# Both MLP matrices by Strassen's seven products: the second one too, with its split combinations of features written to DRAM by the first

## The chip, the cores and the metric

One core of a Trainium2 chip runs the whole program. Its engines are TensorE (PE, with its weight loads, PEld), VectorE (DVE), ScalarE (ACT), GpSimd (POOL) and SyncE (SP, which here only issues transfers); 16 DMA engines move data between DRAM and the on-chip SBUF. Matmul results go to PSUM, here eight banks of 128 x 512 fp32. The metric is device time of one execution in microseconds, less is better.

## The reference

One block of a sequence model: x is 512 tokens of 2048 features. Two mixers (HGRN2 and Hyena, not touched here) are followed by an MLP with a squared relu, and a final RMS norm:

```python
def _sq_relu_mlp(u, w1, w2):
    return jnp.square(jax.nn.relu(u @ w1)) @ w2

x = x + g1 * mix_lat
x = x + g2 * _sq_relu_mlp(_modulate(_rmsnorm(x, norm2_g[layer]), sh2, sc2), w_mlp1[layer], w_mlp2[layer])
...
return _rmsnorm(x, final_norm_g)
```

`w_mlp1` is 2048 x 8192, `w_mlp2` is 8192 x 2048, all in fp32. h = relu(u w1)² has 8192 features for each of 512 tokens.

## The kernel before

**Precision.** Every fp32 operand is split into a high part (a cast to fp32r on ScalarE) and a low part (the rest, a subtraction on VectorE). A product is three matmuls: high x high, high x low, low x high (`mm3`, L265-268). Weights come as pieces of 128 x 1024 (512 KB) on SP's queue; `wsplit` (L214-220) makes `whi` (ScalarE, L218) and `wlo` (VectorE, L161, the line of every tensor-tensor operation) in three buffers each. `take` (L1188) hands the next split piece to PE and calls `ahead`, which emits the splits three pieces on; the table `loads` says at which piece which transfer is issued.

**First matrix, feature-major.** h comes in 32 sets of 256 features. Set 0 is plain. For sets 1 to 31 the product of the 2 x 2 blocks of w1 and of x is made by Strassen's scheme with seven products instead of eight: P1, P2, P6, P5, P7, P3, P4, each 8 x 3 = 24 matmuls of 128 x 256, thus 168 a set. The combinations of x (tiles `U`, seven for each of 8 feature groups) are made once before the loop, by `u_plain` and `u_sums` (L1082-1092: casts L1079, L1089, sums `cb` L1088, differences L161). The sums of weights (`wsum`, `raw<-raw`) are made for each set on VectorE. The four results of a set come from PSUM through `s` (copies on ScalarE) and `c` (sums on VectorE), and `store_h` (L1200) squares them and stores the set as fp32, 512 KB, to `hd[s]` on ScalarE's queue.

**Second matrix, plain.** Two passes over the features, one for each half of the 2048 outputs. A step `q` reads one set of h back (`load_h`, L1172, SP's queue, 512 KB), splits it (`hs`: ScalarE L1280, VectorE L161), takes two weight pieces (`load_w2`, `prep_w2`) and makes 4 token blocks x 2 halves x 2 x 3 = 48 matmuls of 128 x 512 in `down` (L1294-1304); 64 steps. The eight banks sum over a whole pass. `evacuate` (L1306) then makes x + g2 · result, and `final` (L1284) the norm and the stores.

**Order.** The program is written in one order and each engine runs its own instructions in that order; a wait in front of one instruction holds all behind it on that engine. The tile framework places semaphores and moves nothing but by the positions of `take` and the hooks.

Of the kernel before, what the change touches and what calls it, by code (L numbers as in the profile page):

```python
# [154 lines left out]
def body(nc, tc, A, out, stack, dbg, stop):  # L155
# [38 lines left out]
    hd = [DR.tile([P, 1024], F32, name=f"hd{s_}") for s_ in range(DFF // 256)]  # L194
# [870 lines left out]
    def u_plain(q):  # L1065

        ca = cas[q] = ca_tile(q)
        for j in range(2):
            kb = 2 * q + j
            xp = bank(2 * (q % 2) + j)  # L1070
            for i in range(4):
                pe.transpose(xp[:, i * P:(i + 1) * P], x1[i][:, kb * P:(kb + 1) * P], ident)
            act.activation(out=ca[:, 2 * j:2 * j + 2].rearrange("p a t -> p (a t)"), in_=xp, func=AF.Identity,
                           scale=gn2[:, kb:kb + 1], bias=sh2[:, kb:kb + 1])
        if q == 7:
            close("R")
            pools["X"] = pool("X", side=right)
        u = U[q] = (UP if q < 7 else pools["X"]).tile([P, 2, 7, 256], F32R, tag=f"u{q}", name=f"u{q}")
        act.copy(u[:, 0, 0:4], ca)  # L1079
        tt(u[:, 1, 0:4], ca, u[:, 0, 0:4].bitcast(F32), ALU.subtract)  # L1080

    def u_sums(q):  # L1082

        ca, u = cas.pop(q), U[q]
# [4 lines left out]
        act.copy(u[:, 0, 4:7], cb[:, 0:3])  # L1089
        tt(u[:, 1, 4:7], cb[:, 0:3], u[:, 0, 4:7].bitcast(F32), ALU.subtract)  # L1090
        act.copy(u[:, 0, 0], cb[:, 3])
        tt(u[:, 1, 0], cb[:, 3], u[:, 0, 0].bitcast(F32), ALU.subtract)
# [27 lines left out]

    def prep_set(s):
# [18 lines left out]
        def p3():  # L1140
            tt(st[1], st[1], raws[s][1], ALU.add)
            return split(st[1])
        return [lambda: split(raws[s][0]), lambda: split(raws[s][1]), p6, lambda: split(st[0]), p7, p3,
                lambda: split(raws[s][3])]


    w2 = mlp2_order()
    N1 = 7 * (NS - 1)
    WLAST = 4
    preps = [f for s in range(1, NS) for f in prep_set(s)]  # L1150
    loads = {7 * (s - 2): [lambda s=s: load_set(s)] for s in range(2, NS)}
    raw2, hraw = {}, {}

    def load_w2(t):
        if t < 2:
            raw2[t] = YM.tile([P, 1024], F32, tag=f"ym{8 + t}", name="w2raw")
        else:
            raw2[t] = wraw()
        dma(raw2[t], A["tiles"][mlp_tile[w2[t]]])

    def prep_w2(t):
        raw = raw2.pop(t)
        if t < len(w2) - WLAST:
            hi, lo = wsplit(raw)
        else:
            hi = pools["V"].tile([P, 1024], F32R, tag=f"xhi{t % WLAST}", name="xhi")
            lo = pools["V"].tile([P, 1024], F32R, tag=f"xlo{t % WLAST}", name="xlo")
            act.copy(hi, raw)
            tt(lo, raw, hi.bitcast(F32), ALU.subtract)
        return tuple(v.rearrange("p (k n) -> p k n", k=2) for v in (hi, lo))  # L1170

    def load_h(q):  # L1172
        hraw[q] = pools["X"].tile([P, 2, 512], F32, tag=f"hr{q % 2}", name="hraw")
        dma(hraw[q].rearrange("p a t -> p (a t)"), hd[q % NS])

    preps += [lambda t=t: prep_w2(t) for t in range(len(w2))]
    for t in range(len(w2)):
        loads.setdefault(7 * (NS - 2) if t < 2 else N1 + t - 3, []).append(lambda t=t: load_w2(t))
    for q in range(2 * NS):
        loads.setdefault(7 * (NS - 2) if q < 1 else N1 + 2 * q - 4, []).append(lambda q=q: load_h(q))  # L1180
# [7 lines left out]
    def take():  # L1188
        g = at[0]
        for f in loads.pop(g, ()):  # L1190
            f()
# [4 lines left out]
    def c_tile():  # L1196
        return YM.tile([P, 4, 256], F32, tag=f"ym{12 + c_tile.n % 2}", name="c")
    c_tile.n = 0

    def store_h(s, c):  # L1200

        act.activation(out=c, in_=c, func=AF.Square)
        mdma(hd[s], c.rearrange("p a t -> p (a t)"))
        c_tile.n += 1
# [4 lines left out]
    for q in range(8):  # L1209
# [19 lines left out]
    c = c_tile()  # L1229
# [4 lines left out]
    def xs_(tag):  # L1234
        return pools["X"].tile([P, 256], F32, tag=tag, bufs=2, name=tag)

    def product(ps, name, start):
        hi, lo = take()
        i = SLOT[name]
        for q in range(8):  # L1240
            mm3(ps, hi[:, q], lo[:, q], U[q][:, 0, i], U[q][:, 1, i], start and q == 0, q == 7)

    for s in range(1, NS):
        X, Y, Z = (bank(3 * (s % 2) + i)[:, 0:256] for i in range(3))
        c = c_tile()
# [12 lines left out]
        tt(c[:, 2], X, s5, ALU.add)
        act.activation(out=c[:, 2], in_=c[:, 2], func=AF.Relu, scale=-1.0)
        product(Z, "P3", False)  # L1260
        tt(c[:, 0], Z, s2, ALU.add)
        act.activation(out=c[:, 0:2], in_=c[:, 0:2], func=AF.Relu)
        product(X, "P4", False)
        act.activation(out=c[:, 3], in_=X, func=AF.Relu, scale=-1.0)
        store_h(s, c)


    close("U")
    pools["V"] = pool("V")
    rows2 = [YM.tile([P, 2, 512], F32, tag=f"ym{12 + ng}", name="rows2") for ng in range(4)]  # L1270
    grs = [t[:, 0] for t in rows2]
    ss3 = pools["V"].tile([P, 4, 4], F32, name="ss3")
    x1 = [pools["V"].tile([P, D], F32, name=f"x1b{i}") for i in range(4)]
    hs = {}

    def split_h(q):
        for j in range(2):
            pl, tag, nb_ = (YM, f"ym{10 + j}", 1) if q == 0 else (pools["V"], f"hs{j}", 3)
            t = pl.tile([P, 2, 512], F32R, tag=tag, bufs=nb_, name="hs")
            act.copy(t[:, 0], hraw[q][:, j])  # L1280
            tt(t[:, 1], hraw[q][:, j], t[:, 0].bitcast(F32), ALU.subtract)
            hs[q, j] = t

    def final(i0):  # L1284

        r = rstd(pools["V"], ss3[:, i0:i0 + 2], 2, f"r3{i0}")
        for ng in range(4):
            for i in range(2):
                sl = slice(ng * 512, (ng + 1) * 512)
                t = x1[i0 + i][:, sl]  # L1290
                vec.scalar_tensor_tensor(out=t, in0=t, scalar=r[:, i:i + 1], in1=rows2[ng][:, 1], op0=ALU.mult, op1=ALU.mult)
                dma(out[0, (i0 + i) * P:(i0 + i + 1) * P, sl], t)

    def down(q, w_, toks):  # L1294
        for g, (hi, lo) in enumerate(w_):
            for i in toks:
                sl = slice(i * P, (i + 1) * P)
                ps = psb[4 * g + i]
                for j in range(2):
                    t = hs[q, j]  # L1300
                    first, last = q % NS == 0 and j == 0, q % NS == NS - 1 and j == 1
                    pe.matmul(ps, t[:, 0, sl], hi[:, j], start=first, stop=False, skip_group_check=True)  # L1302
                    pe.matmul(ps, t[:, 0, sl], lo[:, j], start=False, stop=False, skip_group_check=True)  # L1303
                    pe.matmul(ps, t[:, 1, sl], hi[:, j], start=False, stop=last, skip_group_check=True)  # L1304

    def evacuate(p, toks):  # L1306
        for g in range(2):
            for i in toks:
                residual(pools["V"], psb[4 * g + i], i, 2 * p + g, ss3)

    split_h(0)
    NL, late = WLAST // 2, []
    for q in range(2 * NS):
        if q % NS == 0:
            psb = [bank(i) for i in range(8)]
        if q + 1 < 2 * NS:
            split_h(q + 1)
        if q == 1:
            for ng in range(4):
                sl = slice(ng * 512, (ng + 1) * 512)  # L1320
                mdma(rows2[ng][:, 0], grow[1:2, sl].broadcast_to([P, 512]))
                mdma(rows2[ng][:, 1], A["final_norm_g"][:, sl].broadcast_to([P, 512]))
            for i in range(4):
                for ng in range(4):
                    mdma(x1[i][:, ng * 512:(ng + 1) * 512], xd[i][ng])
        if q < 2 * NS - NL:
            down(q, [take(), take()], range(4))
            if q == NS - 1:
                evacuate(0, range(4))
        else:  # L1330
            late.append([take(), take()])
            down(q, late[-1], (0, 1))
# [21 lines left out]
```

## Time and profile before

| | us |
|---|---|
| runs: median (lowest, highest) | 2824.98 (2822.47, 2828.32) |
| the profiled execution: time | 2819.74 |
| its span | 2818.0 |
| first matrix, sets 1 to 31 (1460 to 2087 us of the span) | 627 |
| second matrix (2087 to 2803 us) | 716 |
| last matmul to the end | 15 |

In the lines below, "busy" is time in which an engine works on data; what it issues (transfers, semaphores) isn't counted. PE's matmuls are pipelined: the duration of one in a record is longer than the distance between two, so the cost of one is the length of a window without idle time divided by its count. The figure behind a bar, with an arrow, is idle time of the engine in front of that group and what ended it.

### The profile page before, as it was taken

To read this page: it belongs to the slowest core of one execution; us is meant where nothing else is said; L and a number is where in the kernel's file an instruction comes from. 1 tells how busy PE (TensorE), PEld (TensorE's weight loads), DVE (VectorE), ACT (ScalarE), POOL (GpSimd) and SP (SyncE) were. 2 spreads that over 40 slices of the span, in tenths; PEclk is the share of its full clock that TensorE was granted. 3 is DMA by queue.
4 is the path that set the end of the run, shared out by engine and by line. 5 is a ranking of instruction groups with operands and counts; after the bars stand their busy time and mean duration, and the time that the engine had idled before them with its cause. 6 is when DMAs were issued, how large, how long until landed. Compare 5 with 4: busy or idle time off the path is not lost.

```text
span 2818.0 us, 38644 instructions
## 1 busy us (share of the span) xinstructions
PE 2752.9 (98%) x15676; PEld 2291.4 (81%) x15676; DVE 1553.5 (55%) x2109; ACT 1118.7 (40%) x1588; POOL 20.2 (1%) x42
## 2 busy tenths in 40 slices
PE   7999999999999999999979999999999999999997
PEld 2468888787888778878769999999998888888886
DVE  4448777745555556433377777777753333433335
ACT  5432223444344334522275555555542232322222
POOL 0000000000000000000000000000000000000000
PEclk9999999999999999999989999999999999999999
DMA  8676555713333344325334343434354444444442
GB/s 307 216 259 204 166 181 170 247 57 113 124 124 113 120 131 144 109 88 209 114 111 138 128 136 127 137 127 137 127 200 162 140 137 145 139 142 138 146 142 105
DMA packets 138399, 419.77 MB, mean 149 GB/s; under 512 B 15483, under 2 KB 15867, under 8 KB 136556
## 3 DMA queue, kind: packets, MB, share of 16 engines
q1 hardware_dynamic: 119520, 364.17, 39.6%
q10 hardware_dynamic: 15500, 39.76, 3.8%
q0 software_dynamic: 3200, 13.37, 1.3%
q8 instruction: 123, 2.02, 0.3%
q14 instruction: 56, 0.46, 0.1%
HBM read 382.88 MB, written 34.36 MB: 148 GB/s over the span
## 4 chain that ended last, share of the span: by engine, by line
PE 89%; DVE 4%; DMA 4%; ACT 2%; issue 1%; SPq 0%; DVEq 0%; ACTq 0%; POOLq 0%
PE bank L266 17%; PE bank L267 17%; PE bank L268 17%; PE bank L1304 8%; PE bank L1302 8%; PE bank L1303 8%; DMA ga<-ada_dram 2%; PE bank L1039 2%; PE bank L1041 2%; PE bank L1040 2%; PE bank L487 2%; PE bank L937 1%; PE bank L939 1%; DVE gacc L570 1%; DVE wlo L161 1%
## 5 line engine op out<-in xcount | busy, mean ns | idle before, releaser
L161 DVE TENSOR_TENSOR wlo<-raw,whi 128x1024 fp32r<-128x1024 f32 (+1 forms) x336 | 408.6, 1216 | 498.8 <-ACT whi L218 480.5
L218 ACT CAST whi<-raw 128x1024 fp32r<-128x1024 f32 (+1 forms) x336 | 350.4, 1043 | 725.1 <-PE bank L267 265.1
L266 PE MATMUL bank<-u,whi 128*128 128x256 f32 (+1 forms) x1768 | 503.0, 286 | 7.0 <-ACT u L1089 5.6
L267 PE MATMUL bank<-u,whi 128*128 128x256 f32 (+1 forms) x1768 | 506.6, 287 | 2.5 <-DVE u L161 2.5
L268 PE MATMUL bank<-u,wlo 128*128 128x256 f32 (+1 forms) x1768 | 504.5, 286 | 0.0
L268 PE MATMUL bank<-uT,wlo 128*128 128x512 f32 x1024 | 408.4, 399 | 0.0
L267 PE MATMUL bank<-uT,whi 128*128 128x512 f32 x1024 | 408.0, 398 | 0.0
L266 PE MATMUL bank<-uT,whi 128*128 128x512 f32 x1024 | 407.7, 399 | 0.0
L1303 PE MATMUL bank<-wlo,hs 128*128 128x512 f32 x992 | 392.3, 395 | 0.0
L1304 PE MATMUL bank<-whi,hs 128*128 128x512 f32 x992 | 392.3, 395 | 0.0
L1302 PE MATMUL bank<-whi,hs 128*128 128x512 f32 x992 | 391.5, 395 | 0.0
L266 PEld LDWEIGHTS bank<-u,whi 128*128 128x128 f32 x1768 | 339.3, 192 | 10.3 <-ACT u L1089 6.4
L267 PEld LDWEIGHTS bank<-u,whi 128*128 128x128 f32 x1768 | 339.7, 192 | 5.7 <-DVE u L161 4.5
L268 PEld LDWEIGHTS bank<-u,wlo 128*128 128x128 f32 x1768 | 339.1, 192 | 1.1
L268 PEld LDWEIGHTS bank<-uT,wlo 128*128 128x128 f32 x1024 | 193.2, 189 | 52.0 <-issue 12.7
L1304 PEld LDWEIGHTS bank<-whi,hs 128*128 128x128 f32 x992 | 186.5, 188 | 44.9
L1303 PEld LDWEIGHTS bank<-wlo,hs 128*128 128x128 f32 x992 | 186.5, 188 | 44.9
L1302 PEld LDWEIGHTS bank<-whi,hs 128*128 128x128 f32 x992 | 186.5, 188 | 44.9
L266 PEld LDWEIGHTS bank<-uT,whi 128*128 128x128 f32 x1024 | 193.3, 189 | 36.3 <-issue 9.2
L267 PEld LDWEIGHTS bank<-uT,whi 128*128 128x128 f32 x1024 | 193.3, 189 | 33.1 <-issue 6.8
L570 DVE SCALAR_TENSOR_TENSOR gacc<-ga,sil,gacc 128x512 f32<-128x512 f32 x240 | 179.2, 747 | 63.7 <-DMA ga<-ada_dram 61.2
L161 DVE TENSOR_TENSOR hs<-hraw,hs 128x512 fp32r<-128x512 f32 x128 | 87.8, 688 | 186.2 <-ACT hs L1280 186.1
(434 smaller groups left out, 3606.7 us busy)
## 6 DMA issues: line engine op xcount, KB each, us to landing
raw<-tiles_dram SPq DMA_DIRECT2D x332, 512.0 KB, 3.6
ga<-ada_dram SPq DMA_DIRECT2D x256, 256.0 KB, 3.4
wa<-ada_dram SPq DMA_DIRECT2D x64, 512.0 KB, 6.7
hraw<-hd SPq DMA_DIRECT2D x64, 512.0 KB, 4.7
rawe<-tiles_dram SPq DMA_DIRECT2D x60, 512.0 KB, 3.6
hd<-c ACTq DMA_DIRECT2D x32, 512.0 KB, 2.7
rawo<-tiles_dram SPq DMA_DIRECT2D x16, 512.0 KB, 3.5
x<-x_dram SPq DMA_DIRECT2D x4, 1024.0 KB
```

The costliest lines, as they stand in the source:

```text
L161: tt = lambda o, x, y, op: vec.tensor_tensor(out=o, in0=x, in1=y, op=op)
L218: act.copy(hi[:, :n], raw[:, :n])
L266: pe.matmul(ps, wh, xh, start=start, stop=False, skip_group_check=True)
L267: pe.matmul(ps, wh, xl, start=False, stop=False, skip_group_check=True)
L268: pe.matmul(ps, wl, xh, start=False, stop=stop_, skip_group_check=True)
L487: pe.matmul(gm[32 * j:32 * j + 32, :], sil[:, kk], w_[kk // 2][:, kk % 2].rearrange("p a n -> p (a n)"), start=kk < 4, stop=kk >= 12, skip ...
L570: vec.scalar_tensor_tensor(out=acc, in0=g, scalar=s, in1=acc, op0=ALU.mult, op1=ALU.add)
L1039: pe.matmul(ps, m[:, 0, sl], hi[:, k], start=first, stop=False, skip_group_check=True)
L1040: pe.matmul(ps, m[:, 0, sl], lo[:, k], start=False, stop=False, skip_group_check=True)
L1302: pe.matmul(ps, t[:, 0, sl], hi[:, j], start=first, stop=False, skip_group_check=True)
L1303: pe.matmul(ps, t[:, 0, sl], lo[:, j], start=False, stop=False, skip_group_check=True)
L1304: pe.matmul(ps, t[:, 1, sl], hi[:, j], start=False, stop=last, skip_group_check=True)
```

## The change

The second matrix goes by the same seven products, token-major: the stationary operand is now a block of 128 tokens of h (a combination), the moving one 512 columns of a combination of weights. Eight rounds t: a group of 2048 features (t // 2) and a half of the outputs (t % 2). A round has seven products, each of 4 weight pieces x 2 x 2 token blocks x 3 = 48 matmuls of 128 x 512; each product's two banks are added into a sum `y` (512 x 2048 fp32) in SBUF by `add_up` (L1353), with one or two targets.

- `store_h` makes the combinations of h when a set is done: the square, three sums (`sums`, L1086), the split of three plain and four summed blocks (`va`, `vb`), and seven stores of 256 KB on POOL's queue instead of one of 512 KB on ScalarE's. `hd` is 4 x 7 arrays of 128 x 4096: h's split combinations, both parts, 58.7 MB in all. The transfers are declared float32r on both sides.
- `load_slot` (L1185) reads them back in halves of 1 MB (rows of 8 KB) into four buffers on POOL's queue, two for each product, 112 in all. Nothing of h is split in the second stage.
- `load_piece` loads 16 weight pieces a round on SP's queue; `weight_sum` makes their sums on VectorE (16 a round), `split2` splits 28 pieces a round. 
- The last set of the first matrix runs its products in another order (P1, P6, P5, P7, P2, P3, P4), so that the tiles of x's sums (`UB`, `X2`) come free after P7; there `start_mlp2` opens a pool and issues the first transfers of the second stage. A21 and A22 follow when `UA` is free, after P4.
- `finish` and `final` do the residual and the norm on `y`; `c` has one buffer instead of two, the copies `s` one instead of two.

The core of the diff:

```diff
+def mlp2_tile(t, n, k, j):
+    return ("w_mlp2", 16 * (t // 2) + 4 * j + k, (t % 2) * 1024 + n * 512, 2, 2)
-    hd = [DR.tile([P, 1024], F32, name=f"hd{s_}") for s_ in range(DFF // 256)]
+    hd = [[DR.tile([P, 4096], F32, name=f"hd{w}_{i}") for i in range(7)] for w in range(4)]
+    def order1(s):
+        return ("P1", "P2", "P6", "P5", "P7", "P3", "P4") if s < NS - 1 else ("P1", "P6", "P5", "P7", "P2", "P3", "P4")
+    ORDER2 = ("P1", "P2", "P6", "P5", "P7", "P4", "P3")
+    SLOT2 = dict(P1=0, P3=1, P2=2, P5=3, P7=4, P6=5, P4=6)
+    def load_slot(t, pi):
+        for hf in range(2):
+            v = pools["Z1"].tile([P, 4, 2, 256], F32R, tag=f"sl{nslot2[0] % 4}", name="slot")
+            nslot2[0] += 1
+            pdma(v.rearrange("p q a t -> p (q a t)"),
+                 hd[t // 2][SLOT2[ORDER2[pi]]][:, hf * 2048:(hf + 1) * 2048].bitcast(F32R))
+            slots[t, pi, hf] = v
+    def start_mlp2():
+        for j in range(4):
+            load_piece(0, "A12", j)
+        load_slot(0, 0)
+        load_slot(0, 1)
+    def hooks2(t, pi, j):
+        n = ORDER2[pi]
+        if j == 0 and (t, pi) != (0, 0):
+            nt, np_ = divmod(7 * t + pi + 1, 7)
+            if nt < 8:
+                load_slot(nt, np_)
+        if n == "P1":
+            weight_sum("W1", "A21", "A22", j)
+        elif n == "P2":
+            weight_sum("W2", "W1", "A11", j)
+        elif n == "P6":
+            weight_sum("A21", "A21", "A11", j)
+        elif n == "P7":
+            weight_sum("W2", "W2", "A12", j)
+        if t < 7:
+            for r in {"P6": ("A11",), "P7": ("A12", "A21"), "P4": ("A22",)}.get(n, ()):
+                load_piece(t + 1, r, j)
     def take():
         g = at[0]
-        for f in loads.pop(g, ()):
+        for f in hooks.pop(g, ()):
             f()
         ahead(g + WB)
     def store_h(s, c):
         act.activation(out=c, in_=c, func=AF.Square)
-        mdma(hd[s], c.rearrange("p a t -> p (a t)"))
+        cb = sums(c)
+        va = pools["X"].tile([P, 3, 2, 256], F32R, tag="va", name="va")
+        vb = pools["X"].tile([P, 4, 2, 256], F32R, tag="vb", name="vb")
+        for v, x in ((va, c[:, 1:4]), (vb, cb)):
+            act.copy(v[:, :, 0], x)
+            tt(v[:, :, 1], x, v[:, :, 0].bitcast(F32), ALU.subtract)
+        for i in range(7):
+            v = va[:, i] if i < 3 else vb[:, i - 3]
+            pdma(hd[s // 8][i][:, s % 8 * 512:(s % 8 + 1) * 512].bitcast(F32R), v.rearrange("p a t -> p (a t)"))
-    close("U")
-    pools["V"] = pool("V")
+    close("UA")
+    pools["Z2"] = pool("Z2")
+    for j in range(4):
+        load_piece(0, "A21", j)
+        load_piece(0, "A22", j)
+    y = [pools["Z2"].tile([P, D], F32, name=f"y{i}") for i in range(4)]
+    def add_up(ps, m, n, t, first):
+        for a, (i, sl, _) in enumerate(quarter(m, n, t)):
+            if first:
+                act.activation(out=y[i][:, sl], in_=ps[a], func=AF.Copy, scale=-1.0 if n else 1.0)
+            else:
+                tt(y[i][:, sl], y[i][:, sl], ps[a], ALU.subtract if n else ALU.add)
...
+            for j in range(4):
+                hi, lo = take()
+                for k in range(2):
+                    q = 2 * j + k
+                    h = st[q // 4][:, q % 4]
+                    for a in range(2):
+                        sl = slice(a * P, (a + 1) * P)
+                        first = n in ("P1", "P2", "P5", "P4") and q == 0
+                        pe.matmul(ps[a], h[:, 0, sl], hi[:, k], start=first, stop=False, skip_group_check=True)
+                        pe.matmul(ps[a], h[:, 0, sl], lo[:, k], start=False, stop=False, skip_group_check=True)
+                        pe.matmul(ps[a], h[:, 1, sl], hi[:, k], start=False, stop=q == 7, skip_group_check=True)
+            if n in ("P1", "P2"):
+                add_up(ps, m, 0, 0, w == 0 and n == "P1")
...
+                elif n == "P4":
+                    finish(1, 0, 0)
+                    finish(1, 1, 0)
+                    final(2)
+                    finish(1, 1, 1)
+                elif n == "P3":
+                    finish(1, 0, 1)
+                    final(0)
```

**Order on VectorE in the first loop.** Before, from one set's split of P3 to its successor's (`wsum` sums of weights, `c` results, `wlo` splits):

```order
L161 TENSOR_TENSOR wsum_17080<-wsum_17080,raw 128x1024
L161 TENSOR_TENSOR wlo<-wsum_17078,whi 128x1024
L161 TENSOR_TENSOR c<-bank_17067,s_17110 128x256
L161 TENSOR_TENSOR wlo<-raw,whi 128x1024
L161 TENSOR_TENSOR wsum_17306<-rawe 128x1024
L161 TENSOR_TENSOR rawe<-rawe 128x1024
```

After, at the same place (`cb` the sums of a finished set's h, `va` and `vb` the low parts of its plain and summed blocks):

```order
L163 TENSOR_TENSOR wsum_18710<-wsum_18710,rawe 128x1024
L163 TENSOR_TENSOR cb<-c 128x512
L163 TENSOR_TENSOR va<-c,va 128x3x256
L1091 SCALAR_TENSOR_TENSOR cb<-c,cb 128x256
L163 TENSOR_TENSOR wlo<-wsum_18708,whi 128x1024
L1091 SCALAR_TENSOR_TENSOR cb<-c,cb 128x256
L163 TENSOR_TENSOR wsum_18893<-raw,rawo 128x1024
L163 TENSOR_TENSOR c<-bank_18697,s_18740 128x256
L163 TENSOR_TENSOR vb<-cb,vb 128x4x256
L163 TENSOR_TENSOR wlo<-rawe,whi 128x1024
```

Five operations of the set before stand in front of the next set's splits; a set has 19 rows instead of 14.

**Order on VectorE where the second stage begins.** Before, with the last `c` of set 31, then the first pieces of w2 and h:

```order
L161 TENSOR_TENSOR wlo<-w2raw,whi 128x1024
L161 TENSOR_TENSOR c<-bank_18436,s_18536 128x256
L161 TENSOR_TENSOR wlo<-w2raw,whi 128x1024
L161 TENSOR_TENSOR hs<-hraw,hs 128x512 x2
L161 TENSOR_TENSOR wlo<-raw,whi 128x1024
```

After (`a_18948` to `a_18954` are the pieces A11 of the first round, `a_19209` to `a_19223` A21 and A22 in turn, `sumW` their sums):

```order
L163 TENSOR_TENSOR wlo<-a_18950,whi 128x1024
L163 TENSOR_TENSOR wlo<-a_18952,whi 128x1024
L163 TENSOR_TENSOR cb<-c 128x512
L1091 SCALAR_TENSOR_TENSOR cb<-c,cb 128x256
L163 TENSOR_TENSOR va<-c,va 128x3x256
L1091 SCALAR_TENSOR_TENSOR cb<-c,cb 128x256
L163 TENSOR_TENSOR wlo<-a_18954,whi 128x1024
L163 TENSOR_TENSOR sumW_19240<-a_19209,a_19211 128x1024
L163 TENSOR_TENSOR vb<-cb,vb 128x4x256
```

The sum of the first A21 and A22 stands in front of the last set's `vb` and of every split of A12 (which follow).

**Order on POOL there.** Before, POOL issues nothing after the 16 stores of x (`xd`). After, with the seven stores of set 30, the halves of the first products, and the stores of set 31:

```order
L1262 DMA hd_6_131<-vb 128x512
L1189 DMA slot<-hd_0_104 128x2048 x2
L1189 DMA slot<-hd_2_106 128x2048 x2
L1262 DMA hd_0_125<-va 128x512
L1262 DMA hd_1_126<-va 128x512
L1262 DMA hd_2_127<-va 128x512
L1189 DMA slot<-hd_5_109 128x2048
L1262 DMA hd_3_128<-vb 128x512
```

The halves of P1 and P2 (`hd_0`, `hd_2`) go ahead of set 31's stores, the second half of P6 (`hd_5`) goes behind them.

More of the change, by code (lines that the diff above doesn't have):

```diff
@@ L1151, in body @@
[L1151 to L1180, printed above, removed]
+    ORDER2 = ("P1", "P2", "P6", "P5", "P7", "P4", "P3")
@@ new lines, in split2, with weight_sum @@
+    def split2(role, j):
+        return tuple(v.rearrange("p (k n) -> p k n", k=2) for v in wsplit(pieces[role, j]))
+    def weight_sum(o, x, y_, j):
+        if o not in ("A21",) and (o, x) != ("W2", "W2"):
+            pieces[o, j] = piece_tile(o, j, "sum" + o)
+        tt(pieces[o, j], pieces[x, j], pieces[y_, j], ALU.add)
+    def start_mlp2():
[20 more added lines that the diff above has]
+                load_piece(t + 1, r, j)
@@ new lines, in body @@
+    preps = [f for s in range(1, NS) for f in prep_set(s)]
+    hooks = {7 * (s - 2): [lambda s=s: load_set(s)] for s in range(2, NS)}
+    hooks.setdefault(N1 - 7, []).append(lambda: [load_piece(0, "A11", j) for j in range(4)])
+    for t in range(8):
+        for pi, n in enumerate(ORDER2):
+            for j in range(4):
+                hooks.setdefault(N1 + 28 * t + 4 * pi + j, []).append(lambda t=t, pi=pi, j=j: hooks2(t, pi, j))
+                r = dict(P1="A11", P2="A12", P6="W2", P5="W1", P7="A21", P4="A22", P3="W2")[n]
+                preps.append(lambda r=r, j=j: split2(r, j))
@@ L1284, in final, with load_x1, load_fr @@
+    def load_x1(m):
+        for i in range(4):
+            t = x1b[m, i] = piece_tile(("A11", "A12")[m], i, "x1b")
+            for n in range(2):
+                mdma(t[:, n * 512:(n + 1) * 512], xd[i][2 * m + n])
+    def load_fr():
+        for j in range(2):
+            t = piece_tile("A21", j, "fr")
+            mdma(t, A["final_norm_g"][:, j * 1024:(j + 1) * 1024].broadcast_to([P, 1024]))
+            fr.append(t)
     def final(i0):
-        r = rstd(pools["V"], ss3[:, i0:i0 + 2], 2, f"r3{i0}")
+        r = rstd(GP, ss3[:, i0:i0 + 2], 2, f"r3{i0}")
@@ L1289, in final @@
                 sl = slice(ng * 512, (ng + 1) * 512)
-                t = x1[i0 + i][:, sl]
-                vec.scalar_tensor_tensor(out=t, in0=t, scalar=r[:, i:i + 1], in1=rows2[ng][:, 1], op0=ALU.mult, op1=ALU.mult)
+                t = y[i0 + i][:, sl]
+                vec.scalar_tensor_tensor(out=t, in0=t, scalar=r[:, i:i + 1],
+                                         in1=fr[ng // 2][:, ng % 2 * 512:(ng % 2 + 1) * 512], op0=ALU.mult, op1=ALU.mult)
                 dma(out[0, (i0 + i) * P:(i0 + i + 1) * P, sl], t)
[L1294 to L1332, printed above, removed]
```

179 lines of the change are left out of this document (113 added, 66 removed).

## The prediction

> **What bounds the kernel now.** I read the page first, then windows of the two loops of the MLP, then groups by line. The page gives busy time, share of the span and instructions of each engine:
>
> ```profile
> span 2818.0 us, 38644 instructions
> PE 2752.9 (98%) x15676; PEld 2291.4 (81%) x15676; DVE 1553.5 (55%) x2109; ACT 1118.7 (40%) x1588; POOL 20.2 (1%) x42
> PE 89%; DVE 4%; DMA 4%; ACT 2%; issue 1%; SPq 0%; DVEq 0%; ACTq 0%; POOLq 0%
> ```
>
> The third line is the chain that ended last: TensorE carries 89% of it. So fewer matmuls are worth their time, as long as the others keep up stage by stage. The windows show the stages. Columns: window and length, then busy us (count) of PE, PEld, DVE, ACT and POOL, then the granted clock, the DMA share and GB/s.
>
> ```profile
> 1600.00:1700.00 100.00, 100.00 (x837) 100.00 (x837) 72.11 (x70) 51.18 (x69) 0.00 (x0) 1.00 0.40 130
> 2200.00:2400.00 200.00, 200.00 (x859) 161.15 (x858) 66.69 (x71) 56.87 (x71) 0.00 (x0) 1.00 0.43 142
> 2087.00:2803.00 716.00, 716.00 (x3074) 577.34 (x3072) 257.84 (x295) 213.85 (x281) 0.00 (x0) 1.00 0.43 145
> 1267.00:1287.00 20.00, 20.00 (x89) 16.41 (x88) 6.12 (x5) 5.79 (x6) 2.62 (x5) 1.00 0.92 369
> 10.00:25.00 15.00, 5.88 (x10) 1.92 (x10) 7.16 (x11) 11.88 (x13) 0.00 (x0) 1.00 1.02 421
> ```
>
> The first is the loop of the first matrix: no idle PE, 100/837 = 0.1195 us a matmul, so a set of 168 takes 20.1 us, with VectorE busy 72%. The next two are the second matrix: no idle PE, full clock, 716/3074 = 0.233 us a matmul, VectorE only a third busy. The last two are the fullest DMA stretches of this trace: 369 to 421 GB/s. Both MLP loops are bound by PE alone.
>
> **What goes: matmuls.** The second matrix has 64 steps of 48 now, and the groups show that they are all alike (128x512):
>
> ```profile
> L1303 PE MATMUL bank<-wlo,hs 128*128 128x512 f32 x992 | 392.3, 395 | 0.0
> L1304 PE MATMUL bank<-whi,hs 128*128 128x512 f32 x992 | 392.3, 395 | 0.0
> L1302 PE MATMUL bank<-whi,hs 128*128 128x512 f32 x992 | 391.5, 395 | 0.0
> ```
>
> (96 more read `xhi` or `xlo`.) Their 395 ns are pipelined; the 0.233 us from the window is what one costs. After, there are 8 rounds of 7 products of 48 = 2688 of the same shape, with one weight load each as before. 3072 − 2688 = 384, and 384 × 0.233 = **−89.5 us**; the stage becomes 2688 × 0.233 = 626 us, 78.3 a round.
>
> **What the first loop gets.** Each set gains five VectorE operations (512, 256, 256, 768 and 1024 elements) and two ScalarE casts (768, 1024). The same forms stand in the trace where the sums of x are made:
>
> ```profile
> L161 DVE TENSOR_TENSOR u<-ca,u 128x1024 fp32r<-128x1024 f32 x8 | 9.8, 1224 | 6.7 <-ACT u L1079 6.7
> L161 DVE TENSOR_TENSOR u<-cb,u 128x768 fp32r<-128x768 f32 x8 | 7.6, 955 | 2.1 <-ACT u L1089 2.0
> L1088 DVE SCALAR_TENSOR_TENSOR cb<-ca,cb 128x256 f32<-128x256 f32 x16 | 6.8, 422 | 0.3
> L161 DVE TENSOR_TENSOR cb<-ca 128x512 f32<-128x512 f32 x8 | 5.5, 690 | 3.3 <-ACT ca L1073 3.1
> L1079 ACT CAST u<-ca 128x1024 fp32r<-128x1024 f32 x8 | 8.4, 1054 | 0.1
> L1089 ACT CAST u<-cb 128x768 fp32r<-128x768 f32 x8 | 6.7, 838 | 9.5 <-DVE cb L1088 9.5
> ```
>
> VectorE: 0.69 + 2 × 0.42 + 0.96 + 1.22 = 3.7 us a set. It has 0.72 × 20.1 = 14.5 now, so 18.2 of 20.1 (91%). ScalarE: 0.51 × 20.1 = 10.3 plus 1.9 = 12.2 (61%). The total fits under PE, and the splits stand up to three weight tiles ahead (3 × 2.87 us of PE), while the new operations that stand in front of any one split sum to 3.7. I take **+1 us**. Below: 0, since PE does not wait there now. Above: the 28% that VectorE idles now are mostly waits for results and for ScalarE's casts; if none of them shrank, a set would take 20.1 + 3.7 and 31 sets +115 us. The nearest row is the window with no PE idle at 72%, so I stay near zero.
>
> The seven stores of 256 KB replace one of 512 KB, on POOL's queue instead of ScalarE's:
>
> ```profile
> L1045 POOL DMA_DIRECT2D xd<-x x16 | 8.7, 541 | 132.4 <-DVE x L161 131.6 <-issue 0.3
> xd<-x POOLq DMA_DIRECT2D x16, 256.0 KB, 2.5
> hd<-c ACTq DMA_DIRECT2D x32, 512.0 KB, 2.7
> x<-x_dram POOLq DMA_DIRECT2D x4, 1024.0 KB, 9.6
> ```
>
> Issuing costs POOL 7 × 0.54 = 3.8 us a set, on an engine with nothing else to do. The bytes add 1.84 − 0.52 MB in 20.1 us, 65 GB/s on 130: hidden. The cover is the free half of the DMA engines.
>
> **What the second loop gets.** VectorE, a round: 28 weight splits and 16 weight sums of 1024 elements (44 × 1.22 = 53.7) and 16 sums from PSUM of 512 (0.68 each, 10.9): 65 of 78.3 us. ScalarE: 28 casts × 1.05 = 29.4. Both are under PE.
>
> DMA is where the load grows. A round reads 14 halves of 1.05 MB = 14.7 MB of split h on POOL's queue, and 16 weight pieces, 8.4 MB, on SP's: 23.1 MB in 78.3 us = **295 GB/s**, against 142 now. The two full windows carried 369 and 421; the first is the nearest, since POOL's 1 MB loads and SP's 512 KB loads shared the engines there. Scaled otherwise, 142 GB/s at a share of 0.43 would be 330 GB/s at 1.0. All three exceed 295, and a half is asked for about a product and a half (some 17 us) before its use against 9.6 us to land. I take **0**; with 330 there is a tenth to spare, and loads that come in lumps could cost 20 to 35 us. That is the far end for plain transfers.
>
> But no row here is of a transfer whose two sides are both declared float32r, as the new loads and stores are, so its speed is unknown. A floor is nothing lost (rate as in the 369 window). For a ceiling I let such bytes pass at half of 413 (421 at a share of 1.02): 14.7/0.206 + 8.4/0.413 = 71.2 + 20.3 = 91.5 us a round, 732 for eight, **+106**. I take the floor: element size and bytes are the same on both sides.
>
> The Trainium skill, page "DMA: Bandwidth & Descriptors", section "SWDGE vs HWDGE vs iDMA", states that a float32r destination always counts as a cast, which only GpSimd's route does. It gives no rate for that, and no run here shows one. By the page alone the new transfers are thus another kind than all those in the rows; by the rows the sum stays with 0.
>
> **The seam.** The pieces A21 and A22 of the first round get their memory when PE has made its last product from the first loop's x (P4 of set 31). On VectorE their sums stand ahead of the splits of A12, which the second product needs 11.2 us after the loop begins. In flight then: four A12 pieces and two halves (asked for three products, 8.6 us, earlier), two more halves, eight pieces: 2.1 + 2.1 + 2.1 + 4.2 = 10.5 MB, at 0.42 MB/us 25 us. So the last piece comes about 16 us into the loop, a sum and a split add 2.4, and the splits follow one another: PE stands about 8 to 10 us. What a stand costs beside itself shows here:
>
> ```profile
> 1414.36 0.92 PE L1072 MATMUL bank<-ident,x 128*128 128x128 f32 x3 [7.07 <-DVE x L1100]
> 1412.30:1419.10 6.80, 4.74 (x22) 4.42 (x22) 2.95 (x10) 5.75 (x10) 0.00 (x0) 0.50 0.28 96
> ```
>
> After 7.1 us idle the granted clock was 0.50 for 6.8 us, so 3.4 us lost. I take **+10 and +3**; ends: 0, if the bytes were there in time, and +25, if nothing arrives before all 10.5 MB.
>
> **The tail.** Now:
>
> ```profile
> 2803.13 1.28 DVE L161 TENSOR_TENSOR x1b<-x1b,t 128x512 f32<-128x512 f32 x2
> 2807.12 0.36 DVE L161 TENSOR_TENSOR ss<-ss 128x4 f32<-128x4 f32 x2 [0.19 <-ACT jk L1016]
> 2809.16 5.39 DVE L1291 SCALAR_TENSOR_TENSOR x1b<-x1b,r,rows 128x512 f32<-128x512 f32 x8
> out_dram<-x1b SPq DMA_DIRECT2D x16, 256.0 KB, 2.3
> ```
>
> The last matmul starts at about 2802.9 (the window to 2803 holds it), 15.1 us before the end. After the change VectorE still has, behind that matmul, two or three scalings of the other half (2.0), two sums (1.3), four of the residual (2.6), ScalarE's square (0.8), the root's chain (2809.16 − 2807.12 = 2.0), eight scalings (5.4) and the last store (3.4): 17.5. **+2.5 us**, 0 to +6.
>
> **Sum.** −89.5 + 1 + 0 + 13 + 2.5 = −73. The profiled execution took 2819.74 (1.7 beyond its span) and would become 2747. The median of the runs is 2824.98, 5.2 above it; I keep that offset: **2752**.
>
> **Rivals.**
> - *The float32r transfers are slow and the second loop is bound by DMA.* For: 188 of the 295 GB/s would be of a kind that no row shows. Against: the same bytes, rows of 8 KB as in the 1 MB loads that landed in 9.6 us. At half rate: 2752 + 106 = 2858, and 2880 with a worse seam and the lumps: slower. It decides at this point: the loop equals the old when a round takes (716 − 16)/8 = 87.5 us, so 14.7 MB in 87.5 − 20.3, 219 GB/s, 53% of 413.
> - *VectorE becomes the bound of the first loop.* For: 91% busy, in program order, with waits for PSUM and ScalarE between. Against: it works three tiles ahead. A third of the +115: +38, 2790.
> - *Loads are only late in lumps* (330 GB/s or a rate of 0.75 on POOL's queue): +20 to +35, about 2780.
>
> **Chances.** Forecast (2735 to 2768) 0.48; VectorE 0.12; lumps 0.07; these are the 0.67 of faster. Within 0.2% (5.6 us, about what a measurement of this kernel can tell from no change) 0.05; slower 0.28, nearly all of it the first rival, because its unknown decides over more time than the change can gain. The likeliest case's own range is 2735 to 2768; eight in ten need the first rival too: 2735 to 2880.
>
> **What would show it.** Right: the second loop lasts 640 us with 0.233 us a matmul, PE idle almost only in the first round's second product, released by a split; DMA near 300 GB/s; the first loop at 837 matmuls in 100 us with VectorE near 91%. Wrong: PE in the second loop waiting for the halves again and again with the DMA share near 1.0 (first rival); gaps in every set before a product, released by VectorE (second); a gap each time a round's pieces are loaded (third).

## The result, and the profile after

The changed kernel takes **2752.89 us** (median of four runs, 2751.02 to 2754.84) against 2823.9 before (four runs, the three of the table ahead of the prediction and one more): ratio 0.9746, 95% interval 0.9729 to 0.9763. The forecast was 2752.

The page of the changed kernel (busy us, share, count by engine, and the chain that ended last):

```profile
span 2753.1 us, 38777 instructions
PE 2668.5 (97%) x15292; PEld 2223.0 (81%) x15292; DVE 1881.3 (68%) x2477; ACT 1215.2 (44%) x1636; POOL 197.0 (7%) x378
PE 84%; DMA 6%; DVE 5%; ACT 3%; issue 1%; SPq 0%; DVEq 0%; ACTq 0%; POOLq 0%
```

PE's share of the chain fell from 89 to 84%, and DMA's rose from 4 to 6%. The windows of the changed kernel show where; columns as in the prediction (PE, PEld, DVE, ACT, POOL busy, clock, DMA share, GB/s):

```profile
1600.00:1700.00 100.00, 100.00 (x839) 100.00 (x838) 85.47 (x95) 61.16 (x80) 16.95 (x33) 1.00 0.63 192
2300.00:2500.00 200.00, 200.00 (x863) 162.13 (x862) 153.91 (x153) 75.56 (x72) 19.00 (x36) 1.00 0.85 296
2093.80:2735.60 641.80, 630.03 (x2689) 508.37 (x2688) 500.25 (x507) 253.96 (x271) 60.73 (x115) 0.99 0.85 294
2094.00:2174.00 80.00, 68.42 (x276) 54.05 (x275) 53.64 (x51) 31.27 (x35) 9.53 (x18) 0.94 1.01 375
2111.50:2118.30 6.80, 6.80 (x19) 5.39 (x20) 3.09 (x3) 1.05 (x1) 1.70 (x4) 0.62 1.08 404
2170.30:2177.10 6.80, 6.80 (x23) 5.43 (x24) 6.76 (x6) 1.05 (x1) 0.00 (x0) 0.75 0.71 246
2085.30:2121.63 36.33, 28.74 (x148) 24.17 (x147) 18.98 (x21) 14.31 (x17) 7.43 (x14) 0.91 1.04 389
```

In the windows of the first loop and of the body of the second stage PE doesn't idle. Nearly all that was lost stands in the fourth row: the first 80 us of the second stage, with the DMA engines full (share 1.01), PE idle for 11.6 us and the clock down to 0.94, in two pieces (fifth and sixth row; the last row serves the part on the prediction). PE's timeline there shows its four gaps (start, duration, then in brackets the idle time before it and what ended it):

```profile
2111.45 0.79 PE L1408 MATMUL bank<-wlo,slot 128*128 128x512 f32 x1 [6.15 <-DVE wlo L163]
2121.12 0.50 PE L1408 MATMUL bank<-wlo,slot 128*128 128x512 f32 x1 [1.45 <-DVE wlo L163]
2125.18 0.50 PE L1408 MATMUL bank<-wlo,slot 128*128 128x512 f32 x1 [1.00 <-DVE wlo L163]
2170.27 0.50 PE L1408 MATMUL bank<-wlo,slot 128*128 128x512 f32 x1 [3.00 <-DVE wlo L163]
```

By stages, from the starts of matmuls in the two traces (the first row begins behind PE's wait of 3.3 us early in set 1, at 1463.36 and 1470.03 us):

| | before | changed | difference |
|---|---|---|---|
| first matrix, sets 1 to 31 | 623.6 | 623.8 | +0.1 |
| second matrix | 715.9 | 641.8 | −74.1 |
| last matmul to the end | 15.1 | 17.5 | +2.4 |

The sum is −71.6, the difference of the medians −71.0. The two profiled executions differ by less, 2754.84 − 2819.74 = −64.9, since the changed one took 6.7 us more ahead of the first matrix, in instructions that are the same in both kernels (see e5, e10 and e11).

What held the first 80 us is on VectorE's timeline of the changed kernel:

```profile
2098.61 1.22 DVE L163 TENSOR_TENSOR wlo<-a,whi 128x1024 fp32r<-128x1024 f32 x1
2107.90 1.23 DVE L163 TENSOR_TENSOR sumW<-a,a 128x1024 f32<-128x1024 f32 x1 [8.07 <-DMA a<-tiles_dram]
2109.05 1.22 DVE L163 TENSOR_TENSOR vb<-cb,vb 128x1024 fp32r<-128x1024 f32 x1
2110.18 1.22 DVE L163 TENSOR_TENSOR wlo<-a,whi 128x1024 fp32r<-128x1024 f32 x1
2167.85 1.22 DVE L163 TENSOR_TENSOR sumW<-a,a 128x1024 f32<-128x1024 f32 x1 [5.64 <-DMA a<-tiles_dram]
```

The sum of A21 and A22 waits 8.07 us for its pieces. Behind it stand the last set's `vb` and the split of A12 that PE wants at 2105 and gets at 2111.4. The last row is the same thing once more: a sum for the second round waits 5.64 us for its piece, ahead of the split that PE's gap of 3.00 us in the sixth product waits for.

### The profile page after: what moved, and what is told of

It is laid out like the page before. It is cut to its first block, busy times and chain, and to the rows that moved or that the text cites. A ratio compares the mean times of both kernels' runs of the same rounds, so it can differ in the third digit from the quotient of the medians.

```text
span 2753.1 us, 38777 instructions
## 1 busy us (share of the span) xinstructions
PE 2668.5 (97%) x15292; PEld 2223.0 (81%) x15292; DVE 1881.3 (68%) x2477; ACT 1215.2 (44%) x1636; POOL 197.0 (7%) x378
## 3 DMA queue, kind: packets, MB, share of 16 engines
q0 software_dynamic: 51584, 189.55, 20.6%
## 4 chain that ended last, share of the span: by engine, by line
PE 84%; DMA 6%; DVE 5%; ACT 3%; issue 1%; SPq 0%; DVEq 0%; ACTq 0%; POOLq 0%
PE bank L268 17%; PE bank L269 16%; PE bank L270 16%; PE bank L1408 7%; PE bank L1409 7%; PE bank L1407 7%; DMA ga<-ada_dram 3%; PE bank L1041 2%; PE bank L1043 2%; PE bank L1042 2%; PE bank L489 2%; DMA a<-tiles_dram 2%; PE bank L939 1%; PE bank L941 1%; DVE gacc L572 1%
## 5 line engine op out<-in xcount | busy, mean ns | idle before, releaser
L163 DVE TENSOR_TENSOR wlo<-raw,whi 128x1024 fp32r<-128x1024 f32 (+1 forms) x214 | 259.3, 1212 | 229.6 <-ACT whi L220 212.8
L1408 PE MATMUL bank<-wlo,slot 128*128 128x512 f32 x896 | 355.7, 397 | 11.8 <-DVE wlo L163 11.8
L1409 PE MATMUL bank<-whi,slot 128*128 128x512 f32 x896 | 355.2, 396 | 0.0
L1407 PE MATMUL bank<-whi,slot 128*128 128x512 f32 x896 | 355.1, 396 | 0.0
L269 PE MATMUL bank<-ua,whi 128*128 128x256 f32 (+1 forms) x1024 | 293.4, 287 | 1.5 <-DVE ua L163 1.5
L268 PE MATMUL bank<-ua,whi 128*128 128x256 f32 (+1 forms) x1024 | 292.5, 287 | 0.6 <-ACT whi L220 0.5
L270 PE MATMUL bank<-ua,wlo 128*128 128x256 f32 (+1 forms) x1024 | 292.9, 286 | 0.0
L268 PE MATMUL bank<-ub,whi 128*128 128x256 f32 x744 | 211.6, 285 | 6.8 <-ACT ub L1099 5.9
L1408 PEld LDWEIGHTS bank<-wlo,slot 128*128 128x128 f32 x896 | 169.8, 190 | 54.0 <-DVE wlo L163 14.2
L269 PE MATMUL bank<-ub,whi 128*128 128x256 f32 x744 | 211.6, 285 | 1.1 <-DVE ub L163 1.1
L270 PE MATMUL bank<-ub,wlo 128*128 128x256 f32 x744 | 211.2, 284 | 0.0
L163 DVE TENSOR_TENSOR wlo<-a,whi 128x1024 fp32r<-128x1024 f32 x128 | 156.2, 1220 | 77.9 <-ACT whi L220 77.7
L1407 PEld LDWEIGHTS bank<-whi,slot 128*128 128x128 f32 x896 | 169.7, 189 | 39.8
```

The lines of the kernel that those rows point to most:

```text
L163: tt = lambda o, x, y, op: vec.tensor_tensor(out=o, in0=x, in1=y, op=op)
L268: pe.matmul(ps, wh, xh, start=start, stop=False, skip_group_check=True)
L269: pe.matmul(ps, wh, xl, start=False, stop=False, skip_group_check=True)
L270: pe.matmul(ps, wl, xh, start=False, stop=stop_, skip_group_check=True)
L1407: pe.matmul(ps[a], h[:, 0, sl], hi[:, k], start=first, stop=False, skip_group_check=True)
L1408: pe.matmul(ps[a], h[:, 0, sl], lo[:, k], start=False, stop=False, skip_group_check=True)
```

## The experiments

Two questions were left: does the agreement rest on the right reasons (hidden work in the first loop, float32r transfers at the full rate), and what is the seam's loss, order on an engine or bytes? Times of one kernel differ by a few us from one series of runs to the next (medians of the kernel before: 2819.3 to 2823.9), so ratios are to the kernel before in the same series, and the stage times come from the traces. e4, e7, e8 and e10 have one run each.

**e8 and e7: how far does the first loop hide VectorE's work?** `vb`'s low part is made twice (e8) or four times (e7).

```diff
-            tt(v[:, :, 1], x, v[:, :, 0].bitcast(F32), ALU.subtract)
+            for _ in range(4 if v is vb else 1):
+                tt(v[:, :, 1], x, v[:, :, 0].bitcast(F32), ALU.subtract)
```

> Edit: the same with one operation more, 1.14 us a set: VectorE 18.3 of 20.1 us, 91%, the load that the prediction gave the changed kernel. Theory: still hidden, first loop within 3 us of 624 (TensorE 837 to 839 matmuls in 100 us). Rival (waits count in full): +35 us.

> Edit: VectorE makes the low part of the summed blocks (1024 elements) four times instead of once in every set: three operations more, 3 x 1.14 = 3.4 us a set when they follow one another. VectorE is now busy 17.2 of 20.1 us a set, so 20.6 are needed: theory (the added work of the change lay under TensorE, and VectorE decides only from 20.1 us on): the set takes 20.6 us and a little for waits, +15 to +50 us over 31 sets. Rival (VectorE has more room than the busy time shows): under +8. Rival (waits between VectorE and the others count in full): 31 x 3.4 = +100 or more.

The window from 1600 to 1700 us, of e8 first and then of e7:

```profile
1600.00:1700.00 100.00, 100.00 (x839) 100.00 (x838) 90.44 (x101) 60.77 (x81) 18.39 (x35) 1.00 0.65 196
```

```profile
1600.00:1700.00 100.00, 98.33 (x820) 97.93 (x820) 98.78 (x109) 60.06 (x80) 16.80 (x32) 1.00 0.63 190
```

At 90% VectorE costs next to nothing: the loop of e8 takes 624.4 us against 623.8. At 99% it decides: e7's loop takes 643.4 us, +19.7, within the range given, and PE's gaps are 0.83 us in every second set, 41.3 us apart, so a set takes 20.6 us, just what the sum of VectorE's operations says. The change's own 85% has 2.9 us a set to spare.

**e3: what does the float32r declaration cost?** Loads and stores of the combinations are declared fp32 on both sides.

```diff
-            pdma(v.rearrange("p q a t -> p (q a t)"),
-                 hd[t // 2][SLOT2[ORDER2[pi]]][:, hf * 2048:(hf + 1) * 2048].bitcast(F32R))
+            pdma(v.rearrange("p q a t -> p (q a t)").bitcast(F32),
+                 hd[t // 2][SLOT2[ORDER2[pi]]][:, hf * 2048:(hf + 1) * 2048])
...
```

> Edit: the transfers of the split combinations, stores and loads, are declared fp32 on both sides instead of float32r, on the same queue; the bytes are the same. Theory 'declared kind costs nothing' (the changed kernel's rows show 343 GB/s per full share on POOL's queue and 352 on SP's): 0, within 3 us of the changed kernel, and the same landing times (1 MB halves 6.6 us, stores 3.0 and 5.6). Rival 'the declaration makes the transfers slower, and that is only hidden': halves land in under 5.5 us, the DMA share of the second stage falls from 0.85 to 0.75 or less, and the seam's idle time of 11.6 us shrinks by 3 us or more.

Measured 2756.36 us, ratio 0.9776 (0.976 to 0.9791), not faster. The page's DMA rows, of the changed kernel and then of e3 (MB, share of 16 engines over the span; KB, median us to landing):

```profile
q0 software_dynamic: 51584, 189.55, 20.6%
slot<-hd POOLq DMA_DIRECT2D x112, 1024.0 KB, 6.6
hd<-vb POOLq DMA_DIRECT2D x128, 256.0 KB, 5.6
```

```profile
q0 software_dynamic: 37248, 189.55, 18.9%
slot<-hd POOLq DMA_DIRECT2D x112, 1024.0 KB, 6.4
hd<-vb POOLq DMA_DIRECT2D x128, 256.0 KB, 5.1
```

The declaration costs 14336 more packets, 64 for each of the 224 stores, and 9% of the queue's DMA time for the same bytes, but nothing that is waited for. The rival is out: the DMA share of the second stage falls to 0.81, not to 0.75 or less, halves land 0.2 us sooner, not over a microsecond, and the stage's idle time was 14.9 us, not less.

**e4: where would these transfers decide?** Each half is loaded twice.

```diff
             slots[t, pi, hf] = v
+            pdma(v.rearrange("p q a t -> p (q a t)"),
+                 hd[t // 2][SLOT2[ORDER2[pi]]][:, hf * 2048:(hf + 1) * 2048].bitcast(F32R))
```

> Edit: each half of the split combinations is loaded twice into its buffer; a round then reads 29.4 + 8.4 = 37.8 MB instead of 23.1. Theory (float32r loads share the full 413 GB/s; they were hidden, and the point from which they decide is 23.1 MB in 78.3 us): the stage is bound by DMA, 37.8 / 0.413 = 91.5 us a round, 732 for the stage instead of 642, so about +90, 2840 to 2860, with a DMA share of 0.98 or more. If these loads were slower than plain ones (300 GB/s): 29.4 / 0.3 + 8.4 / 0.413 = 118 us a round, +300. If the stage had more in reserve than the share of 0.85 says: under +50.

Bound by DMA as expected, but a miss in size: 2915.26 us, where 2840 to 2860 was expected. The second stage takes 793.6 us, 99.2 a round: 37.8 MB at 381 GB/s, with PE waiting for halves. I had reckoned with 413 GB/s and a stage of 732 us. Window and DMA rows of e4, 2400 to 2800 us:

```profile
2400.00:2800.00 400.00, 344.93 (x1382) 271.07 (x1381) 258.38 (x253) 120.11 (x115) 60.70 (x115) 0.94 1.01 385
q0 software_dynamic: 16491, 120.10, 79.0%
q1 hardware_dynamic: 9216, 33.56, 22.0%
```

120.10 MB in 79.0% of 400 us and 33.56 in 22.0% are both 380 GB/s per full share: the declared loads and the plain ones run alike when they compete. (Where they don't fill the engines, from 2300 to 2500 us, the queue moves 343 GB/s per full share in the changed kernel and 358 in e3.) The limit of the stage as it is mixed is 381 to 385, and the changed kernel uses 296, 77% of it.

**e5, e11 (the changed kernel again) and e10 (the kernel before again).**

> The changed kernel once more, as it is, beside the runs of e6 on the same chip. Both theories: the same stage times as its first profile (second stage 642 us, first loop 624), and a time within 0.3% of 2753; whatever differs more lies ahead of the first matrix.

> The changed kernel beside e9 on the same chip: second stage 642 within 2 us, with the four gaps of its first profile.

> The kernel before once more, with a profile. Theory (the 6.7 us that the changed kernel's first profile took more ahead of the first matrix are spread of that part, whose instructions are the same): the first transposition of x after the 7.1 us gap starts between 1414 and 1422 us; first loop 624 and second stage 716, both within 2. If the change itself lengthened that part, it starts within 1 us of 1414.4.

e5: 2749.79 us, ratio 0.9752 (0.9734 to 0.9769), second stage 643.8; e11: 2749.3, ratio 0.9743 (0.9728 to 0.9757), second stage 641.4; e10's first matmul after the 7.1 us gap starts at 1414.39 (1414.36 in the first profile). That of the changed kernel starts at 1421.17, 1415.04 and 1415.85, and e8's at 1414.54. e10 lands where both of its readings put it, so it doesn't decide. What does is that the changed kernel itself comes within 0.7 us of it: the part ahead of the first matrix has a spread of some 6 us in its three profiles (10 us with the edits below, up to 1424.48 in e9), and the 6.7 us of the first are not a cost of every run. Two profiles of the kernel before are too few to say whether it spreads as well, so a part of that may still come from the change.

**e1: the sums W1 and W2 emitted six pieces later.**

```diff
-        if n == "P1":
-            weight_sum("W1", "A21", "A22", j)
-        elif n == "P2":
-            weight_sum("W2", "W1", "A11", j)
...
+                if pi == 0:
+                    hooks.setdefault(N1 + 28 * t + 6 + j, []).append(lambda j=j: w_sums(j))
```

> Edit: in every round the sums W1 = A21 + A22 and W2 = W1 + A11 are emitted six pieces later, so that on VectorE no sum stands ahead of the first splits of A12. Theory 'order' (the stand at the seam is VectorE waiting for A21 and A22 in front of splits that don't need them): the idle time of TensorE in the second stage, 11.6 us in the changed kernel (6.15, 1.45, 1.00 and 3.00), falls to 4 us or less, no window of half clock is left, and the time falls by 8 to 16 us, to about 2741. Rival 'bytes' (the DMA engines are full at 400 GB/s for the first 80 us of the stage, so TensorE waits for bytes in any order): the pieces land when they did, the wait moves to the third product, more than 8 us of idle time remain, and the time falls by 4 us at most.

Half a miss for both readings: 2744.36 us, ratio 0.9735 (0.9721 to 0.975), the stage 636.3 us with 8.0 us of idle time. The last gaps shrank, but the first stayed at 6.09 us. The trace of e1 still has the first sum, with 8.01 us of waiting, ahead of A12's first split: the tile framework had put it there again (it seems to put first what it holds to be ready), so the edit moved the other sums only. (The section on the kernel says that the framework moves nothing; that is wrong.)

**e2: and g2's row later.**

```diff
-    mdma(g2, grow[1:2, :].broadcast_to([P, D]))
+    hooks.setdefault(N1 + 28 * 5, []).append(lambda: mdma(g2, grow[1:2, :].broadcast_to([P, D])))
```

> Edit: as e1, and the 1 MB row of g2 is loaded five rounds later. It takes 1.05 MB out of the first round's DMA traffic, 2.6 us at 400 GB/s. Theory 'order': within 2 us of e1, since no byte is waited for. Theory 'bytes': 2 to 4 us below e1, and the late pieces land that much sooner.

Ratio 0.9751 (0.9732 to 0.9769), stage 635.9. The framework moved the row's load back to the seam, so e2 is e1 once more and tells nothing of bytes.

**e6: an order that can't be undone.** The first W1 sums take a factor 1.0 that is made from A12's last split.

```diff
+                vec.tensor_scalar(out=gates[0], in0=ready[N1 + 7][1][:, 0, 0:1].bitcast(F32), scalar1=0.0, scalar2=1.0,
+                                  op0=ALU.mult, op1=ALU.add)
...
+            vec.scalar_tensor_tensor(out=pieces["W1", j], in0=pieces["A21", j], scalar=gates[0], in1=pieces["A22", j],
+                                     op0=ALU.mult, op1=ALU.add)
```

> Edit: as e1, and the four sums W1 of the first round take a factor 1.0 that is made from the last split of A12, so that no order can put them ahead of it. Theory 'order': the 6.1 us gap at the start of the second product goes with it; idle time of TensorE in the second stage 1 to 4 us (the fourth W2 split is the one that comes late, by about 2), no half clock; the stage lasts 627 to 631 us instead of 642, and the time is 9 to 14 us below e5. Rival 'bytes': A12 or the second product's halves have not landed either, since the DMA engines are full; the gap stays over 3 us, named after a DMA or ScalarE's cast, and the stage lasts 635 or more.

The gap at the second product is gone, which shows its cause. But another of 6.83 us came at the third, the stage takes 646.0 us, and the time misses the forecast: 2759.64 us, ratio 0.9785 (0.976 to 0.981), no better than e5 beside it. ScalarE's timeline of e6 shows what took over:

```profile
2107.49 1.05 ACT L220 CAST whi<-a 128x1024 fp32r<-128x1024 f32 x1 [1.28 <-PE bank L1422]
2121.15 0.35 ACTq L1358 DMA_DIRECT2D g2row<-grow  x1
2121.62 1.99 ACT L220 CAST whi<-sumW 128x1024 fp32r<-128x1024 f32 x2 [13.09 <-DMA hd<-vb]
```

The load of g2's row sits on ScalarE's queue and takes the memory of `vb`, so it waits for the last stores; W2's casts stand behind it for 13.09 us. In the changed kernel ScalarE waits for the same stores for 4.89 us, up to 2122.49; VectorE's wait had made PE so late that it cost nothing.

**e9 and e12: that wait away as well.** In e9 the row's load was emitted five rounds later with e2's edit, and the second round's sums held too.

```diff
+        if t < 2:
...
+                vec.tensor_scalar(out=gates[0], in0=ready[N1 + 27 * t + 7][1][:, 0, 0:1].bitcast(F32),
...
```

> Edit: as e6, with the factor also in front of the sums W1 of the second round (made there from the third split of A12), and the row of g2 loaded five rounds later, so that ScalarE's queue no longer stands behind the last stores of vb with the casts of W2 behind it (13.1 us in e6). Theory 'order' in its present form (each stand at the seam is an engine's queue held by an instruction that waits for a late transfer): idle time of TensorE in the second stage under 3 us, in gaps under 2 us each, and no half clock; the second stage lasts 625 to 630 us at the pitch of e5 (629 to 633 at that of e6) instead of 642 to 643, and the time is 9 to 16 us below the changed kernel on the same chip. Rival 'bytes': some wait of over 3 us for a piece or a half remains in the first 80 us, stage 634 or more.

A miss: the framework took the load back to the seam, and the same gap stood there with 7.03 us (stage 642.7, ratio 0.9769, 0.9755 to 0.9784). e12 holds the load with a one-column copy from `y`, and the third and fourth sum behind splits of W2:

```diff
+    def load_g2():
+        act.copy(g2[:, 0:1], y[0][:, 0:1])
+        mdma(g2, grow[1:2, :].broadcast_to([P, D]))
+    hooks.setdefault(N1 + 28 * 5, []).append(load_g2)
...
```

> Edit: as e6 (first round's W1 sums held behind the last split of A12), the third and fourth sum held behind the first and third split of W2, the second round's W1 sums behind the second split of its A11, and the load of g2's row held by a one-column copy out of y at the start of round 6 (in e2 and e9 the framework had moved that load back to the seam, where it waited for the last stores and the casts of W2 waited behind it on ScalarE). Theory 'order': no gap of TensorE over 3 us in the second stage, 1.5 to 5 us in all, no half clock; stage 627 to 632 us (642 in the changed kernel), 8 to 14 us below it in time: 0.971 of the kernel before, below e1's 0.9735. Rival 'bytes': a gap of over 3 us stays where a piece or a half has not landed, stage 634 or more.

**2736.22 us, ratio 0.9677 (0.9658 to 0.9696): faster than both kernels.** But only part of that is the seam. PE's gaps in e12's first round:

```profile
2116.01 0.51 PE L1431 MATMUL bank<-wlo,slot 128*128 128x512 f32 x1 [1.32 <-DVE wlo L163]
2124.76 0.80 PE L1430 MATMUL bank<-whi,slot 128*128 128x512 f32 x2 [3.43 <-DMA slot<-hd]
2126.40 0.80 PE L1431 MATMUL bank<-wlo,slot 128*128 128x512 f32 x1 [0.85 <-DVE wlo L163]
```

A wait of over 3 us for a half itself remains, as the rival said, and the stage's idle time is 9.45 us, where 1.5 to 5 were expected. The reading that fits these runs, though none of them isolates it: order decides which wait comes last, bytes how far it can fall. Two windows of e12, the first 80 us and the body of the stage:

```profile
2092.00:2172.00 80.00, 74.10 (x313) 59.42 (x312) 56.81 (x56) 34.41 (x38) 10.04 (x19) 0.96 1.02 382
2300.00:2500.00 200.00, 200.00 (x884) 165.69 (x883) 163.25 (x162) 77.83 (x75) 19.52 (x37) 1.00 0.88 307
```

In e1, e6, e9 and e12 the share is 1.02 in these 80 us, in e3 0.93. The second row is the surprise: 884 matmuls in 200 us against 863, with the same clock of 1.00. (Such a count takes in the matmuls that the window's edges cut, some two too many, so the distances below are those between the starts in that window.) The table splits each stage into the 2687 distances of its matmuls at that length and the rest, which is mostly idle time and lost clock:

| | stage | distance, ns | 2687 of them | rest | idle in 80 us |
|---|---|---|---|---|---|
| changed | 641.8 | 232.4 | 624.4 | 17.4 | 11.6 |
| e1 | 636.3 | 232.4 | 624.4 | 11.9 | 8.0 |
| e6 | 646.0 | 234.3 | 629.5 | 16.5 | 10.5 |
| e9 | 642.7 | 233.3 | 627.0 | 15.7 | 7.8 |
| e12 | 624.5 | 226.7 | 609.1 | 15.4 | 5.9 |

So e12 owes 15.3 of its 17.3 us to the distance of its matmuls and 2.0 to the waits; it halved the idle time of the first 80 us and gave some back in small gaps later. That its stage came out below the 627 to 632 us expected is luck: with the changed kernel's distance it would take 639.8 us, in the rival's range of 634 or more. By the rest, e1 and e2 save most.

## Why the prediction was right

- **Matmuls.** Right: 384 fewer. The starts in the body of the stage are 0.2324 us apart, where the forecast had 0.233, so those that are left take 624.4 us instead of 626.4: another 2.0 us less.
- **First loop, +1.** Measured +0.1. VectorE stands at 85%, not 91%: operations that follow one another start 1.14 us apart, where their records last 1.22, and I had summed the records (those that start from 1600 to 1700 us sum to 90.6 us and cover 85.5). e8 and e7 show that the reason given holds: some 18 us of VectorE's work a set stay hidden, and 20.6 do not. The rival that counted waits in full is out.
- **Transfers, 0.** Right, and for the reason given. 296 GB/s were used, 295 forecast, and PE waited for no half. The Trainium skill's page "DMA: Bandwidth & Descriptors" states in "SWDGE vs HWDGE vs iDMA" that a float32r destination counts as a cast. e3 shows a difference of kind in the stores alone (64 packets more for each; the loads take as many as plain ones), and the rate, which the page leaves open, is the plain one when they compete (e4: 380 and 380 GB/s). The first rival, with the largest chance after the forecast, thus had nothing to stand on; only its point of decision was real, and with 381 instead of 413 GB/s (e4) it lay nearer than I put it.
- **The seam, +13.** Right in place and mechanism for its main part: VectorE's sum of A21 and A22 ahead of A12's splits, 8.6 us of idle time in the second product. The 3.00 us in the sixth product, behind a sum of the second round, were not forecast. The term was mis-sized: the rest of the stage is 17.4 us. Of these, 11.8 are idle time (10 forecast) and 0.38 × 6.8 + 0.25 × 6.8 = 4.3 lower clock, in two windows behind the gaps of 6.15 and 3.00 us (0.62 and 0.75); the forecast was one window and 3. (The row it was read from gives 2.4, not 3.4: PE was busy in only 4.74 of the 6.8 us at half clock.) The step that failed is "10.5 MB, so the last piece comes about 16 us into the loop"; the last sum started at 2121.63, 27.9 us into it. The count left out set 31's seven stores (1.8 MB) and the halves of P6 (2.1 MB), 14.4 MB in all. From the first piece's issue to that sum, 36.33 us, the DMA engines moved 14.1 MB at 389 GB/s (last row of the windows above), about those bytes, at a lower rate than the 420 taken.
- **The tail, +2.5.** Measured 15.1 to 17.5, +2.4, with the operations that were listed.
- **The sum, −73**, came out as −71.6: the seam's 4.4 us too little were met by 2.0 from the matmuls' distance, 0.9 in the first loop and 0.1 in the tail. That part of the agreement is luck.

## What to carry to other kernels

Before trading matmuls for traffic, divide the bytes of a round by its new time and hold that against a long full stretch with the same mix of queues; here 296 of 381 GB/s was hidden, and the doubled traffic of e4 was not. (A short stretch says too much: 421 GB/s over 15 us ahead of the change, 385 over 400 us in e4.) At the seam between two stages count every byte in flight, stores and rows for later included: there the engines are full although the average leaves room. And a transfer on a computing engine's queue that waits for memory holds all of that engine's work behind it; removing the wait in front only shows it (e6).

## What the runs showed that was not expected

The distance of the 128x512 matmuls in the second stage went with the build: 863, 862 and 861 in 200 us for three profiles of the changed kernel, 859 for both of the kernel before, 856, 859 and 884 for e6, e9 and e12, all at a granted clock of 1.00 and with no more than 0.02 us of idle time. The 128x256 matmuls of the first loop moved far less (839 in 100 us in the changed kernel, 836 in e6, e9 and e12). Those three add one, two and four one-column tiles to a pool that is opened ahead of the weights' pool and so, it seems, move the weights' tiles in SBUF; that this is the cause was not tested. It is worth 15.3 us in e12, more than any edit saved at the seam.

The trace of the kernel before speaks for it that the tiles have a part in this. Its last 96 matmuls read the weights from other tiles (`xhi`, `xlo`):

```profile
2759.16 0.39 PE L1303 MATMUL bank<-wlo,hs 128*128 128x512 f32 x1
2781.33 0.39 PE L1302 MATMUL bank<-xhi,hs 128*128 128x512 f32 x1
2802.90 0.39 PE L1304 MATMUL bank<-xhi,hs 128*128 128x512 f32 x1
```

From each of these rows to the next it is 95 distances: 233.4 ns each up to the change of tiles, 227.1 behind it, in one build and with the same shapes. VectorE was idle from 2773 to 2788 us, on both sides of the change, so its work is not the reason. But the tiles can't be all: in the changed kernel the starts are 233.3 ns apart from 2180 to 2240 us and 232.4 from 2300 us on, with the same tiles. What sets the distance stays open.

A gap of 3.00 us was enough to bring the clock to 0.75 over the next 6.8 us (window from 2170.30 above). The Trainium skill, page "TensorE: Matmul & The Clock Gate", section "Why this matters for your kernels", asks for no idle gaps beyond about 3 us. The runs here draw no such line. In e8 a gap of 1.96 us had the same lower clock behind it:

```profile
2165.48 0.50 PE L1409 MATMUL bank<-wlo,slot 128*128 128x512 f32 x1 [1.96 <-DVE wlo L163]
2165.50:2172.30 6.80, 6.80 (x23) 5.44 (x24) 6.14 (x6) 1.05 (x1) 0.00 (x0) 0.75 0.82 289
```

And in e3 one of 2.92 us had none:

```profile
2128.47 0.50 PE L1408 MATMUL bank<-wlo,slot 128*128 128x512 f32 x1 [2.92 <-DVE wlo L163]
2128.50:2135.30 6.80, 6.80 (x29) 5.54 (x30) 6.80 (x8) 2.10 (x2) 0.53 (x1) 1.00 0.38 110
```

So the length of a gap alone did not decide it.
